# Compressed probabilities transposed two heads at a time, 512-column score matmuls, and a new order of the features in a hybrid decoder layer

## The chip, the cores and the metric

The kernel runs on one core of one Trainium2 chip, as one launch. The metric is device microseconds for that launch. The median of three timed runs of the kernel before is 698.51 us (698.43 to 698.52).

## What is computed

The reference is one decoder layer over 512 tokens of width 1024, in float32. The input is normalised and projected once (`w_in`). From the projection come a pooling mixer, an attention mixer and two sigmoid gates that merge them; then follow an output projection, a residual, a second norm, and a gated feed-forward layer with a causal convolution of width 3. The change lies in the attention mixer and in the features that run beside it:

```python
blk = kv[:, idx] + pe[None, None, :, None, :]                 # compress_blocks, for keys and for values
hid = jax.nn.silu(jnp.einsum('bnlgd,ldh->bngh', blk, w1))
return jnp.einsum('bngh,hd->bngd', hid, w2)
...
s = jnp.einsum('bqgrd,bngd->bgrqn', qc, kc) * scale           # 31 compressed keys
p_cmp = masked_softmax(s, cmp_end[None, :] <= t[:, None], -1)
o_cmp = jnp.einsum('bgrqn,bngd->bqgrd', p_cmp.astype(vc.dtype), vc)
...
out = gc[..., 0:1] * o_cmp + gc[..., 1:2] * o_sel + gc[..., 2:3] * o_win
```

There are eight query heads in two groups (`g`). At this length all eight selection blocks are chosen and the window covers everything, so the selected and the window branch are two causal attentions with keys and values of their own.

## The kernel before

Numbers are kept to float32 accuracy by splitting every operand into a rounded high part and a low rest, so that one product is three matmuls: high by high, high by low, low by high. TensorE is PE in the profile, VectorE DVE, ScalarE ACT, GpSimd POOL, and SyncE (SP) issues most DMAs.

**Order.** The kernel doesn't issue instructions as it is written. `Plan` (from line 112) records every operation with an estimated cost. `run` places them engine by engine, `dues` gives each a due time, and `emit` repeats this twelve times (TRIES) and issues the best order found. What comes out is a fixed order per engine; the semaphores between engines follow from the data alone. `pl.behind(op)` adds a dependency that only the planner knows: it moves an operation later in the order, but leaves no wait in the program. All operations pass through line 395 in the end, so the profile is read by tile names (`kt`, `cst`, `mm`), not by lines.

**Two streams.** TensorE work is in two streams that the planner interleaves. Stream "m" is the attention. Stream "f" (inside `with pl.on("f")`) is 22 features, the products of the normalised input with one 128-column slice of `w_in`. Each feature is 24 matmuls of 512 columns, shown as `mm<-xh,whi`, `mm<-xl,whi`, `mm<-xh,wlo`. Features need little of the other engines, so they fill TensorE while the attention waits for VectorE and ScalarE. They are two for the compression (`kc`), four for pooling (`pool_in`, each followed by a `mix`), eight pool gates (`gpy`, with four `pool_out` pairs) and eight attention gates (`thn`). A feature's weights come by an SP load into the ring `wraw` (three buffers), a ScalarE copy into `wlo`, an accumulating POOL DMA onto it, and a ScalarE copy into `whi`.

**The stage of the change.** After the first projections, `rope_split(t)` applies the rotary factors to the queries (`qp`) and keys (`kp`) of token tile t on VectorE and splits them into `qs` and `ks`; `qk_transpose(t)` transposes them on TensorE and ScalarE copies them out as `QT[g, t]` and `KT[0/1, t]` (high over low, and low over high). At the same time the two compression features give `kc` (four VectorE multiplications each), to which POOL adds the position terms, giving `kcb` (two additions each, 128x512). 64 matmuls with `w1` and two with `w2` follow, then a chain of small VectorE instructions (`kcx`, `kcm`, `kct`, `kcsp`), a transposition, and four copies into the zero-padded `kcz`. `cmp_scores` multiplies those with the queries, `cmp_softmax` makes the probabilities, and writes high part, low part and the high part again into `cst` (16 blocks of 3 x 32 columns, a tile for each group). `cmp_transpose(g, i)` transposes the four heads of one token tile into `PTc[g]`, 96 rows. In `av(h, 1)` one matmul multiplies the 96 rows with `vst`, 96 rows of compressed values.

**Scores.** `scores(h, i)` makes, for query tile i, the scores against key tiles 0 to i. For each key tile there are two matmuls of 256 columns (selected and window keys side by side), one against the high over low tile and one against the low over high one. The result goes into the two-bank tile `sc` where there are more than two key tiles, else into one of three `tr` banks.

Of the kernel before, what the change touches and what calls it, by code (L numbers as in the profile page):

```python
# [9 lines left out]
F32R = mybir.dt.float32r  # L10
# [5 lines left out]
P = 128  # L16
T = 512
# [381 lines left out]
def hybrid_layer(ctx: ExitStack, tc: tile.TileContext, xT, pos, par, cst, poolw, w1, wa, wb, wf,  # L399
# [23 lines left out]
    def bank(tag, shape=(P, T)):  # L423
        return pl.tile(ps, shape, F32, tag, tag, {"mm": 2, "tr": 3, "av": 1, "sc": 1}[tag], psum=True)
# [282 lines left out]
    def qk_transpose(t):  # L707
        for g in range(2):
            pt = bank("tr", (P, 4, P))
            with pl.unit():  # L710
                for i in range(4):
                    PE.transpose(pt[:, i], f32(qsp[t][g][:, i].rearrange("p a d -> p (a d)")), ident)
            QT[g, t] = page("qt", (P, 4, P), F32R)
            ACT.activation(QT[g, t], pt, AF.Copy)
        pt = bank("tr", (P, 2, 2, P))
        with pl.unit():
            for g in range(2):
                for b in range(2):
                    PE.transpose(pt[:, g, b], f32(ksp[t][:, 2 * b + g].rearrange("p a d -> p (a d)")), ident)
        KT[0, t], KT[1, t] = (page("kt", (P, 2, 2, P), F32R) for _ in range(2))  # L720
        ACT.activation(KT[0, t], pt, AF.Copy)
        ACT.activation(KT[1, t][0:64], pt[64:128], AF.Copy)
        ACT.activation(KT[1, t][64:128], pt[0:64], AF.Copy)

    rope_split(0)
    rope_split(1)
# [19 lines left out]
    pscale = R("pscale")  # L746
    yph, ypl, pooled = [], [], {}
    with pl.on("f"):
        for i in range(2):
            pt = feature(i, xh, xl)  # L750
            kc = page("kc", (P, 2, 256))
            for g in range(2):
                for q in range(2):
                    DVE.tensor_mul(kc[q * 64:(q + 1) * 64, g], pt[g * 64:(g + 1) * 64, q::2],
                                   rb[g * 64:(g + 1) * 64, q::2])
            for a in range(2):
                b = page("kcb", (P, 2, 32, 8))
                POOL.tensor_add(b.rearrange("p g n l -> p (g n) l"), kc.rearrange("p g (n l) -> p (g n) l", l=8),
                                pe[:, i, 8 * a:8 * a + 8][:, None, :].to_broadcast([P, 64, 8]))
                KC[i, a] = b  # L760
        def pool_in(gi):
# [36 lines left out]

        def pool_out(c):
            wh, wl = weights(wpo[c].rearrange("p a k n -> p (a k n)"), 1024)  # L800
            for f in (2 * c, 2 * c + 1):
                o = (f % 2) * 512
                pt = bank("mm")
                mm3(pt, wh[:, o:o + 512], wl[:, o:o + 512], yph, ypl, 0, 4)
                DVE.scalar_tensor_tensor(gpy[f], gpy[f], 1.0, pt, op0=ALU.add, op1=ALU.mult)
                SP.dma_start(gdr[f], gpy[f])

        pool_in(0)
        pw = page("pw", (P, 4, P))
        with pl.behind(turned[1]):  # L810
            SP.dma_start(pw, poolw)
        split(pwh, pwl, pw)
        for gi in range(1, 4):
            pool_in(gi)
            gate(thn, gi - 1, 14)
            mix(gi - 1)
        gate(thn, 3, 14)
        mix(3)
        for f in (0, 2):
            gate(gpy, f, 6)  # L820
            gate(gpy, f + 1, 6)
            pool_out(f // 2)
        gate(thn, 4, 14)
        for f in (4, 6):
            gate(gpy, f, 6)
            gate(gpy, f + 1, 6)
            pool_out(f // 2)
        for f in range(5, 8):
            gate(thn, f, 14)

    chid = []
    for i in range(2):
# [40 lines left out]
        for z in kcz.values():  # L873
            POOL.memset(f32(z), 0.0)
    pk = compress_out(1)
    vst = keep("vst", (96, 2, DH), F32R)
    for g in range(2):
        src = pk[g * 32:(g + 1) * 32, 0:64]
        for s in range(2):
            ACT.activation(vst[s * 32:(s + 1) * 32, g], src, AF.Copy, scale=0.5)  # L880
        DVE.scalar_tensor_tensor(vst[64:96, g], src, 0.5, f32(vst[g * 32:(g + 1) * 32, g]),
                                 op0=ALU.mult, op1=ALU.subtract)

    def compress_kt():
        pt = bank("tr")
# [11 lines left out]
    cps, cst_ = {}, {}  # L897
    PTc = {g: pl.tile(sb, (96, 4, T), F32R, "ptc", "ptc", 1) for g in range(2)}

    def cmp_scores(g):  # L900
        pt = bank("tr")
# [8 lines left out]
    def cmp_softmax(g):  # L910
        pt = bank("tr", (P, 4, P))
        with pl.unit():
            for hh in range(4):
                PE.transpose(pt[:, hh], cps[g][:, hh], ident)
        e = page("ce", (P, 16, 32))
        e4 = e.rearrange("p (h t) n -> p h (t n)", h=4)
        sm = keep("csm", (P, 3, 16), bufs=2)
        st = cst_[g] = keep("cst", (P, 16, 3, 32), F32R)
        DVE.tensor_add(e4, pt, C("cmask")[:, None, :].to_broadcast([P, 4, P]))
        DVE.tensor_reduce(sm[:, 0], e, axis=AX, op=ALU.min)  # L920
        DVE.tensor_sub(e, e, sm[:, 0][:, :, None].to_broadcast([P, 16, 32]))
        ACT.activation(e, e, AF.Exp, scale=-1.0)
        DVE.tensor_reduce(sm[:, 1], e, axis=AX, op=ALU.add)
        DVE.reciprocal(sm[:, 2], sm[:, 1])
        DVE.tensor_mul(sm[:, 2], sm[:, 2], vg[:, 4 * g:4 * g + 4].rearrange("p h t -> p (h t)"))
        DVE.tensor_mul(e, e, sm[:, 2][:, :, None].to_broadcast([P, 16, 32]))
        ACT.activation(st[:, :, 0], e, AF.Copy)
        ACT.activation(st[:, :, 2], e, AF.Copy)
        DVE.tensor_sub(st[:, :, 1], e, f32(st[:, :, 0]))

    def cmp_transpose(g, i):
        pt = bank("tr", (P, 4, P))
        with pl.unit():
            for hh in range(4):
                PE.transpose(pt[0:96, hh], f32(cst_[g][:, 4 * hh + i].rearrange("p a n -> p (a n)")), ident)
        ACT.activation(PTc[g][:, :, i * P:(i + 1) * P], pt[0:96], AF.Copy)

    Pt, PT, po, Oraw = {}, {}, {}, {}
    Oh = [page("oh", dt=F32R) for _ in range(4)]
# [2 lines left out]
    def scores(h, i):  # L942
# [1 line left out]
        n = i + 1  # L944
        pt = bank("sc", (P, 4, 2, P)) if n > 2 else bank("tr", (P, 2, 2, P))
        with pl.unit():
            for j in range(n):
                for s in range(2):
                    PE.matmul(pt[:, j], QT[g, i][:, hh], KT[s, j][:, g], start=(s == 0 and j % 2 == 0),
                              stop=(s == 1), skip_group_check=True)  # L950
        sm = keep("asm", (P, 4, 2), bufs=4)
        if n > 2:
            pp = [pl.tile(sb, (P, T), F32, "pp", "pp", 10)[:, :n * P].rearrange("p (j k) -> p j k", k=P) for _ in range(2)]
# [35 lines left out]
    def av(h, b):  # L989
# [4 lines left out]
        o = po[h]  # L994
        parts = [(0, 0, 0, 0), (1, 0, 1, 128), (2, 256, 2, 256), (2, 0, 3, 256)]
        if b == 1:
            PE.matmul(o[0:64], vst[:, g], PTc[g][:, h % 4], start=False, stop=False)
            parts = parts[::-1]
        for r, s, j, t0 in parts:
            n = 512 - t0  # L1000
# [433 lines left out]
```

## Time and profile before

| what | value |
|---|---|
| median of three runs | 698.51 us |
| the profiled execution's own time | 698.77 us |
| its span, first to last instruction | 697.0 us |
| DVE busy, share of the span | 481.1 us, 69% |
| ACT busy, share of the span | 436.3 us, 63% |
| POOL busy, share of the span | 103.3 us, 15% |
| granted TensorE clock | 1.00 throughout |
| HBM read and written | 70.27 MB, 6.29 MB |

Times inside the program are counted from the span's start. The stages that matter lie as follows: the first projections to about 54 us, the transpositions of queries and keys among the features to about 77 us, the compression to about 98 us, the attention interleaved with the features to about 270 us, a run of features alone to 284 us, then the merge and the feed-forward layer to the end.

A matmul's row gives its start and a duration that includes the way through the array; matmuls overlap, so the cost of one in a stream is the distance from its start to the next start. "x8" on a row of the timeline means that eight equal instructions are merged. The number in brackets is idle time of the engine before the row, and what ended it.

### The profile page before, as it was taken

What the parts mean: (1) busy time and instruction counts of PE and PEld (TensorE: products, weight loads), DVE (VectorE), ACT (ScalarE), POOL (GpSimd) and SP (SyncE); (2) the same over time, 40 slices, a digit from 0 to 9 for tenths busy, and PEclk for the clock granted to TensorE, in tenths of its full rate; (3) what the DMA queues carried; (4) which work ended last, traced back from release to release, by engine and by line L of the source; (5) the groups of instructions that cost most, each with busy time, mean ns of one, the idle gap of its engine ahead of it and who ended that gap; (6) DMA issues with size and microseconds to landing.
All of it is one profiled execution on the core that took longest, in us unless ns stands there. A gap on an engine that the chain in (4) does not pass through costs nothing.

```text
span 697.0 us, 11326 instructions
## 1 busy us (share of the span) xinstructions
PE 691.3 (99%) x4144; PEld 612.0 (88%) x4144; DVE 481.1 (69%) x1025; ACT 436.3 (63%) x798; POOL 103.3 (15%) x127
## 2 busy tenths in 40 slices
PE   9999999999999999999999999999999999999998
PEld 8898888888888888888888899999999999999987
DVE  5768678888866653685559977777766766776542
ACT  7667568767777663443359757768677766675320
POOL 0011400010011010000013223223122112220000
PEclk9999999999999999999999999999999999999999
DMA  8577344355655558744459787879978867864141
GB/s 297 171 177 207 96 111 107 106 137 122 166 136 152 151 126 240 272 164 136 151 144 233 168 214 174 215 169 198 225 189 180 196 162 168 182 158 108 46 128 61
DMA packets 45703, 113.99 MB, mean 164 GB/s; under 512 B 5328, under 2 KB 6096, under 8 KB 45648
## 3 DMA queue, kind: packets, MB, share of 16 engines
q1 hardware_dynamic: 29664, 76.57, 34.2%
q0 software_dynamic: 15840, 36.71, 29.2%
q8 instruction: 32, 0.52, 0.3%
q14 instruction: 23, 0.19, 0.1%
q10 hardware_dynamic: 144, 0.01, 0.0%
HBM read 70.27 MB, written 6.29 MB: 110 GB/s over the span
## 4 chain that ended last, share of the span: by engine, by line
PE 97%; DVE 2%; issue 0%; ACT 0%; POOL 0%; POOLq 0%
PE mm L395 41%; PE tr L395 31%; PE sc L395 14%; PE av L395 11%; DVE kp L395 1%; DVE kc L395 0%; DVE qp L395 0%; DVE th L395 0%; DVE qs L395 0%; DVE rt L395 0%; DVE ks L395 0%; DVE pml L395 0%; DVE o L395 0%; ACT ks L395 0%; POOL ones L395 0%
## 5 line engine op out<-in xcount | busy, mean ns | idle before, releaser
L395 ACT ACTIVATE whi<-wraw 128x1024 fp32r<-128x1024 f32 (+2 forms) x97 | 98.0, 1011 | 69.5 <-issue 24.6
L395 DVE TENSOR_TENSOR wlo<-wraw,whi 128x1024 fp32r<-128x1024 f32 (+1 forms) x66 | 76.3, 1158 | 16.9 <-ACT whi L395 14.9
L395 POOL DMA_DIRECT2D wlo<-wraw x30 | 26.3, 876 | 327.5 <-ACT wlo L395 257.9
L395 PE MATMUL mm<-xh,whi 128*128 128x512 f32 x176 | 73.0, 415 | 0.1
L395 PE MATMUL mm<-xh,wlo 128*128 128x512 f32 x176 | 69.0, 392 | 0.0
L395 PE MATMUL mm<-xl,whi 128*128 128x512 f32 x176 | 68.9, 392 | 0.0
L395 PE MATMUL mm<-tl,sh 128*128 128x256 f32 x190 | 53.5, 282 | 0.0
L395 PE MATMUL mm<-th,sl 128*128 128x256 f32 x174 | 49.1, 282 | 0.0
L395 PE MATMUL mm<-th,sh 128*128 128x256 f32 x174 | 49.0, 281 | 0.0
L395 ACT ACTIVATE wlo<-wraw 128x1024 fp32r<-128x1024 f32 x30 | 31.8, 1059 | 25.5 <-PE mm L395 16.6
L395 POOL DMA_DIRECT2D sl<-r x36 | 31.1, 863 | 88.0 <-ACT sl L395 66.1
L395 ACT ACTIVATE pp<-pp,asm 128x128 f32<-128x128 f32 (+3 forms) x64 | 35.4, 556 | 9.4 <-DVE asm L395 9.3
L395 PE MATMUL sc<-yh,whi 128*128 128x512 f32 x104 | 40.5, 389 | 0.0
L395 PE MATMUL sc<-yl,whi 128*128 128x512 f32 x104 | 40.5, 389 | 0.0
L395 PE MATMUL sc<-yh,wlo 128*128 128x512 f32 x104 | 40.5, 389 | 0.0
L395 PEld LDWEIGHTS mm<-xh,wlo 128*128 128x128 f32 x176 | 33.0, 188 | 7.5
L395 DVE SCALAR_TENSOR_TENSOR ft<-fg,pr,ft 128x511 f32<-128x511 f32 (+1 forms) x44 | 32.9, 749 | 9.5 <-ACT ft L395 8.8
L395 PEld LDWEIGHTS mm<-xh,whi 128*128 128x128 f32 x176 | 33.2, 188 | 4.7 <-DVE th L395 0.5
L395 PEld LDWEIGHTS mm<-xl,whi 128*128 128x128 f32 x176 | 33.3, 189 | 4.0
L395 PEld LDWEIGHTS mm<-tl,sh 128*128 128x128 f32 x190 | 35.7, 188 | 0.4
L395 PEld LDWEIGHTS mm<-th,sh 128*128 128x128 f32 x174 | 32.7, 188 | 1.1
L395 PEld LDWEIGHTS mm<-th,sl 128*128 128x128 f32 x174 | 32.7, 188 | 0.0
(397 smaller groups left out, 2100.6 us busy)
## 6 DMA issues: line engine op xcount, KB each, us to landing
wlo<-wraw POOLq DMA_DIRECT2D x30, 512.0 KB, 4.6
wraw<-wup SPq DMA_DIRECT2D x26, 512.0 KB, 3.9
wraw<-wf SPq DMA_DIRECT2D x22, 512.0 KB, 3.4
r<-wup SPq DMA_DIRECT2D x36, 256.0 KB, 5.4
sl<-r POOLq DMA_DIRECT2D x36, 256.0 KB, 5.4
wraw<-wdn SPq DMA_DIRECT2D x16, 512.0 KB, 3.7
sl<-s POOLq DMA_DIRECT2D x18, 256.0 KB, 5.5
sl<-wraw POOLq DMA_DIRECT2D x18, 256.0 KB, 4.2
```

The costliest lines, as they stand in the source:

```text
L395: getattr(self.real[o.eng], method)(*a, **kw)
```

## The change

Four things are changed, all before the merge:

- `cst` and `PTc` become one tile for both groups. `cst` holds high and low part once each (2 x 32 columns per head), and `cmp_transpose(g, b)` transposes two heads at a time, 128 rows, with b counting pairs of token tiles. The compressed values go into `vz`, 128 x 128 for each group and head of a pair, with the rows of the other head zero: eight small ScalarE copies and four VectorE instructions instead of four and two, and one POOL memset. The matmul in `av(h, 1)` gets 128 rows and 128 columns of weights instead of 96 and 64.
- Keys of two token tiles share one tile: `qk_transpose` transposes keys at odd t only, eight blocks, and `scores` takes two key tiles in one matmul of 512 columns where there are two.
- The four additions of the position terms are on VectorE instead of POOL, and for the planner behind the last key tile (`turned[3]`).
- The features have a new order: the compression's two stand behind a first attention gate, the other attention gates come between the pooling features, the pool gates and `pool_out` at the end.

```diff
-        pt = bank("tr", (P, 2, 2, P))
-        with pl.unit():
-            for g in range(2):
-                for b in range(2):
-                    PE.transpose(pt[:, g, b], f32(ksp[t][:, 2 * b + g].rearrange("p a d -> p (a d)")), ident)
-        KT[0, t], KT[1, t] = (page("kt", (P, 2, 2, P), F32R) for _ in range(2))
...
+        for g in range(2 if t % 2 else 0):
+            pt = bank("tr", (P, 2, 2, P))
+            with pl.unit():
+                for j in range(2):
+                    for b in range(2):
+                        PE.transpose(pt[:, j, b], f32(ksp[t - 1 + j][:, 2 * b + g].rearrange("p a d -> p (a d)")), ident)
+            hl, lh = (page("kt", (P, 2, 2, P), F32R) for _ in range(2))
+            KT[0, t // 2, g], KT[1, t // 2, g] = hl, lh
+            ACT.activation(hl, pt, AF.Copy)
+            ACT.activation(lh[0:64], pt[64:128], AF.Copy)
+            ACT.activation(lh[64:128], pt[0:64], AF.Copy)
...
-                POOL.tensor_add(b.rearrange("p g n l -> p (g n) l"), kc.rearrange("p g (n l) -> p (g n) l", l=8),
-                                pe[:, i, 8 * a:8 * a + 8][:, None, :].to_broadcast([P, 64, 8]))
+                with pl.behind(turned[3]):
+                    DVE.tensor_add(b.rearrange("p g n l -> p (g n) l"), kc.rearrange("p g (n l) -> p (g n) l", l=8),
+                                   pe[:, i, 8 * a:8 * a + 8][:, None, :].to_broadcast([P, 64, 8]))
...
+        gate(thn, 0, 14)
+        kv_in(0)
+        kv_in(1)
+        gate(thn, 1, 14)
         pool_in(0)
...
+        gate(thn, 2, 14)
         gate(thn, 3, 14)
+        pool_in(1)
+        mix(0)
...
+    with pl.behind(turned[2]):
+        POOL.memset(f32(ct[:, 2]), 0.0)
     for g in range(2):
         src = pk[g * 32:(g + 1) * 32, 0:64]
-        for s in range(2):
-            ACT.activation(vst[s * 32:(s + 1) * 32, g], src, AF.Copy, scale=0.5)
+        for r in range(4):
+            ACT.activation(vz[r * 32:(r + 1) * 32, g, r // 2, 0], src, AF.Copy, scale=0.5)
...
-        ACT.activation(st[:, :, 0], e, AF.Copy)
-        ACT.activation(st[:, :, 2], e, AF.Copy)
-        DVE.tensor_sub(st[:, :, 1], e, f32(st[:, :, 0]))
+        ACT.activation(hi, e, AF.Copy)
+        DVE.tensor_sub(lo, e, f32(hi))
...
+            for q in range(2):
+                for a in range(2):
+                    PE.transpose(pt[:, q, a], f32(cst_[:, 2 * b + a, 2 * q:2 * q + 2].rearrange("p h s n -> p (h s n)")), ident)
+        ACT.activation(PTc[:, 2 * g:2 * g + 2, 2 * b * P:2 * (b + 1) * P], pt.rearrange("p q a t -> p q (a t)"), AF.Copy)
...
-            for j in range(n):
+            for j in range(0, n, 2):
+                m = min(2, n - j)
                 for s in range(2):
-                    PE.matmul(pt[:, j], QT[g, i][:, hh], KT[s, j][:, g], start=(s == 0 and j % 2 == 0),
-                              stop=(s == 1), skip_group_check=True)
+                    PE.matmul(pt[:, j:j + m], QT[g, i][:, hh], KT[s, j // 2, g][:, 0:m], start=(s == 0), stop=(s == 1),
+                              skip_group_check=True)
...
-            PE.matmul(o[0:64], vst[:, g], PTc[g][:, h % 4], start=False, stop=False)
+            PE.matmul(o, vz[:, g, h % 2].rearrange("p s d -> p (s d)"), PTc[:, h // 2], start=False, stop=False)
...
-    extra = {(0, 2 * i + 2): (lambda i=i: cmp_transpose(0, i)) for i in range(NT)}
-    extra.update({(4, 2 * i): (lambda i=i: cmp_transpose(1, i)) for i in range(NT)})
+    extra = {(0, 4 * b + 2): (lambda b=b: cmp_transpose(0, b)) for b in range(2)}
+    extra.update({(4, 4 * b): (lambda b=b: cmp_transpose(1, b)) for b in range(2)})
```

From the merge on, TensorE's instructions stand in the same order in both programs.

More of the change, by code (lines that the diff above doesn't have):

```diff
@@ L714, in qk_transpose @@
             ACT.activation(QT[g, t], pt, AF.Copy)
-        pt = bank("tr", (P, 2, 2, P))
-        with pl.unit():
-            for g in range(2):
-                for b in range(2):
-                    PE.transpose(pt[:, g, b], f32(ksp[t][:, 2 * b + g].rearrange("p a d -> p (a d)")), ident)
-        KT[0, t], KT[1, t] = (page("kt", (P, 2, 2, P), F32R) for _ in range(2))
-        ACT.activation(KT[0, t], pt, AF.Copy)
-        ACT.activation(KT[1, t][0:64], pt[64:128], AF.Copy)
-        ACT.activation(KT[1, t][64:128], pt[0:64], AF.Copy)
+        for g in range(2 if t % 2 else 0):
[9 more added lines that the diff above has]
+            ACT.activation(lh[64:128], pt[0:64], AF.Copy)
     rope_split(0)
@@ L748, in hybrid_layer, with kv_in @@
     with pl.on("f"):
-        for i in range(2):
+        def kv_in(i):
             pt = feature(i, xh, xl)
@@ L812, in hybrid_layer @@
         split(pwh, pwl, pw)
[L813 to L816, printed above, removed]
+        gate(thn, 2, 14)
         gate(thn, 3, 14)
-        mix(3)
[L819 to L829, printed above, removed]
+        pool_in(1)
+        mix(0)
+        gate(thn, 4, 14)
+        gate(thn, 5, 14)
+        pool_in(2)
+        mix(1)
+        gate(thn, 6, 14)
+        gate(thn, 7, 14)
+        pool_in(3)
+        mix(2)
+        gate(gpy, 0, 6)
+        gate(gpy, 1, 6)
+        mix(3)
+        pool_out(0)
+        gate(gpy, 2, 6)
+        gate(gpy, 3, 6)
+        pool_out(1)
+        gate(gpy, 4, 6)
+        gate(gpy, 5, 6)
+        pool_out(2)
+        gate(gpy, 6, 6)
+        gate(gpy, 7, 6)
+        pool_out(3)
     chid = []
@@ L875, in hybrid_layer @@
     pk = compress_out(1)
-    vst = keep("vst", (96, 2, DH), F32R)
+    ct = keep("cst", (P, 3, T), F32R)
+    cst_ = ct[:, 0:2].rearrange("p a b -> p (a b)").rearrange("p (t h s n) -> p t h s n", t=4, h=4, s=2)
+    vz = ct[:, 2].rearrange("p (g r s d) -> p g r s d", g=2, r=2, s=2)
+    with pl.behind(turned[2]):
+        POOL.memset(f32(ct[:, 2]), 0.0)
     for g in range(2):
         src = pk[g * 32:(g + 1) * 32, 0:64]
-        for s in range(2):
-            ACT.activation(vst[s * 32:(s + 1) * 32, g], src, AF.Copy, scale=0.5)
-        DVE.scalar_tensor_tensor(vst[64:96, g], src, 0.5, f32(vst[g * 32:(g + 1) * 32, g]),
-                                 op0=ALU.mult, op1=ALU.subtract)
+        for r in range(4):
+            ACT.activation(vz[r * 32:(r + 1) * 32, g, r // 2, 0], src, AF.Copy, scale=0.5)
+        for r in range(2):
+            DVE.scalar_tensor_tensor(vz[r * 64:r * 64 + 32, g, r, 1], src, 0.5, f32(vz[g * 32:(g + 1) * 32, g, 0, 0]),
+                                     op0=ALU.mult, op1=ALU.subtract)
     def compress_kt():
@@ L895, in compress_kt @@
                                AF.Copy)
-    cps, cst_ = {}, {}
-    PTc = {g: pl.tile(sb, (96, 4, T), F32R, "ptc", "ptc", 1) for g in range(2)}
+    cps = {}
+    PTc = pl.tile(sb, (P, 4, T), F32R, "ptc", "ptc", 1)
     def cmp_scores(g):
@@ L917, in cmp_softmax @@
         sm = keep("csm", (P, 3, 16), bufs=2)
-        st = cst_[g] = keep("cst", (P, 16, 3, 32), F32R)
+        hi, lo = (cst_[:, :, :, s].rearrange("p t h n -> p h t n") for s in range(2))
         DVE.tensor_add(e4, pt, C("cmask")[:, None, :].to_broadcast([P, 4, P]))
@@ L926, in cmp_softmax, with cmp_transpose @@
         DVE.tensor_mul(e, e, sm[:, 2][:, :, None].to_broadcast([P, 16, 32]))
-        ACT.activation(st[:, :, 0], e, AF.Copy)
-        ACT.activation(st[:, :, 2], e, AF.Copy)
-        DVE.tensor_sub(st[:, :, 1], e, f32(st[:, :, 0]))
-    def cmp_transpose(g, i):
-        pt = bank("tr", (P, 4, P))
+        e = e.rearrange("p (h t) n -> p h t n", h=4)
+        ACT.activation(hi, e, AF.Copy)
+        DVE.tensor_sub(lo, e, f32(hi))
+    def cmp_transpose(g, b):
+        pt = bank("tr", (P, 2, 2, P))
         with pl.unit():
-            for hh in range(4):
-                PE.transpose(pt[0:96, hh], f32(cst_[g][:, 4 * hh + i].rearrange("p a n -> p (a n)")), ident)
-        ACT.activation(PTc[g][:, :, i * P:(i + 1) * P], pt[0:96], AF.Copy)
+            for q in range(2):
+                for a in range(2):
+                    PE.transpose(pt[:, q, a], f32(cst_[:, 2 * b + a, 2 * q:2 * q + 2].rearrange("p h s n -> p (h s n)")), ident)
+        ACT.activation(PTc[:, 2 * g:2 * g + 2, 2 * b * P:2 * (b + 1) * P], pt.rearrange("p q a t -> p q (a t)"), AF.Copy)
     Pt, PT, po, Oraw = {}, {}, {}, {}
```

## The prediction

> **What bounds the kernel now.** I read the page first, then the waits of TensorE, then busy time by stage.
>
> ```profile
> span 697.0 us, 11326 instructions
> PE 691.3 (99%) x4144; PEld 612.0 (88%) x4144; DVE 481.1 (69%) x1025; ACT 436.3 (63%) x798; POOL 103.3 (15%) x127
> ...
> PE 97%; DVE 2%; issue 0%; ACT 0%; POOL 0%; POOLq 0%
> ```
>
> TensorE is busy 99% of the span and carries 97% of the chain that ended last. So time is won in two ways only: fewer or shorter matmuls, or less of the 697.0 − 691.3 = 5.7 us in which TensorE is idle. The waits that the profile names:
>
> ```profile
> PE tr L395 <- DVE rt L395: 1.3, 1, 1.3
> PE mm L395 <- POOL ones L395: 1.0, 1, 1.0
> ```
>
> ```profile
> 98.00:145.00 47.00, 47.00 (x279) 40.77 (x279) 38.83 (x121) 35.26 (x80) 3.45 (x4) 1.00 0.41 102
> 145.00:270.00 125.00, 124.80 (x687) 104.56 (x686) 83.72 (x255) 86.29 (x175) 13.15 (x15) 1.00 0.58 147
> 270.00:697.00 427.00, 423.83 (x2618) 382.45 (x2616) 288.16 (x439) 249.84 (x421) 72.49 (x84) 1.00 0.68 171
> ```
>
> The second wait is the start of the program, untouched. The first lies in the stage of the change. The windows (length, then busy time of PE, PEld, DVE, ACT and POOL, granted clock, DMA share, GB/s) show the attention without idle TensorE: 47.00 of 47.00 and 124.80 of 125.00 us. The 3.2 us after 270 us belong to the feed-forward part, whose TensorE order the change leaves alone. So what can be gained is the one wait plus matmul time, and everything else that changes is a risk of new waits.
>
> **The wait at 72 us, and what makes it.** Timelines of TensorE, VectorE and GpSimd:
>
> ```profile
> 72.08 0.39 PE L395 MATMUL mm<-xh,wlo 128*128 128x512 f32 x1
> 73.81 0.41 PE L395 MATMUL tr<-cs,qs 128*128 128x128 f32 x2 [1.35 <-DVE rt L395]
> ```
>
> ```profile
> 61.89 0.42 DVE L395 TENSOR_TENSOR kp<-kp,gkv 128x256 f32<-128x256 f32 x1
> ...
> 67.05 1.19 DVE L395 TENSOR_TENSOR kp<-kp,rt 128x64 f32<-128x64 f32 x1
> ...
> 70.79 2.31 DVE L395 TENSOR_TENSOR kp<-kp,gkv 128x256 f32<-128x256 f32 x1
> ...
> 73.25 0.42 DVE L395 TENSOR_TENSOR qs<-qp,qs 128x256 fp32r<-128x256 f32 x1
> ...
> 74.07 0.22 DVE L395 TENSOR_TENSOR kp<-kp,rt 128x64 f32<-128x64 f32 x1
> ...
> 77.02 1.15 DVE L395 TENSOR_TENSOR vg<-gates,cs 128x32 f32<-128x32 f32 x1
> ```
>
> ```profile
> 66.84 1.32 POOL L395 TENSOR_TENSOR kcb<-kc,pr 128x512 f32<-128x512 f32 x1 [2.21 <-DVE kc L395]
> ...
> 71.22 1.60 POOL L395 TENSOR_TENSOR kcb<-kc,pr 128x512 f32<-128x512 f32 x1
> 72.45 1.76 POOL L395 MEMSET kcz<- 128x512 f32 x3
> 76.82 2.52 POOL L395 TENSOR_TENSOR kcb<-kc,pr 128x512 f32<-128x512 f32 x2 [2.61 <-DVE kc L395]
> ```
>
> TensorE waits for `qs`, which VectorE made at 73.25. Ahead of it the multiplication of `kp` took 2.31 us; the same shape took 0.42 at 61.89. It ends at 73.10, just after GpSimd's addition (71.22 + 1.60 = 72.82). The final addition of `kp` took 1.19 instead of 0.22 and ends at 68.24, after the other addition at 68.16; `vg` is a third. Each time a VectorE instruction with two SBUF inputs is held until the GpSimd addition is over. The two before the wait cost 1.89 + 0.97 = 2.86 us of VectorE. With `qs` that much earlier, the idle 1.35 us are gone; counted in starts, 73.81 − 72.08 − 0.23 = 1.50 us.
>
> The Trainium skill states the same as an exclusive lock, and says that a two-input VectorE instruction loses only against a GpSimd instruction that reads SBUF (SBUF — State Buffer, section "SBUF: two separate sides"). By that rule the new memset of `vz` cannot hold VectorE, and the trace agrees: the instructions at 73.25 and 74.07 keep their 0.42 and 0.22 us beside the memsets of 72.45. Were the rule wrong for memsets, the added one would cost at most its own length.
>
> **Terms of the sum.** Spacing is read from the start of a row to the start of the next.
>
> ```profile
> 94.42 3.79 PE L395 MATMUL tr<-qt,kcz 128*128 128x512 f32 x16
> 98.05 0.64 PE L395 MATMUL tr<-kt,qt 128*128 128x256 f32 x4
> ...
> 101.74 1.12 PE L395 MATMUL sc<-kt,qt 128*128 128x256 f32 x8
> 102.69 0.40 PE L395 MATMUL mm<-xh,whi 128*128 128x512 f32 x1
> ...
> 114.15 0.60 PE L395 MATMUL tr<-cs,cst 128*96 128x128 f32 x4
> 114.51 0.47 PE L395 MATMUL mm<-xh,whi 128*128 128x512 f32 x1
> 114.82 0.39 PE L395 MATMUL mm<-xl,whi 128*128 128x512 f32 x1
> 115.05 0.39 PE L395 MATMUL mm<-xh,wlo 128*128 128x512 f32 x1
> ```
>
> ```profile
> L395 PE MATMUL sc<-kt,qt 128*128 128x256 f32 x112 | 16.1, 284 | 0.0
> L395 PE MATMUL tr<-kt,qt 128*128 128x256 f32 x48 | 8.6, 287 | 0.0
> L395 PE MATMUL tr<-cs,cst 128*96 128x128 f32 x32 | 4.8, 272 | 0.0
> L395 PE MATMUL tr<-cs,qs 128*128 128x128 f32 x32 | 4.5, 273 | 1.3 <-DVE rt L395 1.3
> ```
>
> 1. Transpositions of the probabilities: 32 become 16. Four of them and the 512-column matmul behind take 114.82 − 114.15 = 0.67 us, less 0.23 for the latter (115.05 − 114.82) leaves 0.44, or 0.11 each. Sixteen fewer save **1.75 us**. The width grows from 96 to 128; the query transpositions, of 128 rows, have the same duration (273 ns on average against 272), so the rest cost no more.
> 2. Scores: 112 + 48 = 160 matmuls of 256 columns become 64 of 512 and 32 of 256. Eight of 256 take 102.69 − 101.74 = 0.95 us, 0.119 each. One of 512 takes (98.05 − 94.42)/16 = 0.227 at best and 0.23 among the features. A merged pair saves 0.238 − 0.23 = 0.008 to 0.238 − 0.227 = 0.011 us; 64 pairs save 0.5 to 0.7, and I take **0.6 us**. The lower bound is nothing, if wider moving tiles stream no faster per column.
> 3. The wait at 72 us: **1.5 us**, bounds 0 and 1.5.
> 4. The matmul with `vz` streams 512 columns as with `vst`, the key transpositions remain 16: nothing.
>
> The Trainium skill's formula for the gap between isolated matmuls, N/2.4 + 2.5 ns (TensorE: Matmul & The Clock Gate, section "Back-to-back issue gap"), would make the merge worth 2.5 ns a pair, 0.16 us in all; the spacing here is 10 ns above it for 256 columns. The difference of 0.4 us lies inside the range.
>
> What is added elsewhere, and its cover. Counts for the changed program are from the order in which its instructions stand on each engine.
>
> ```profile
> L395 DVE TENSOR_TENSOR ps<-u 128x511 f32<-128x511 f32 x4 | 2.7, 686 | 0.1
> L395 DVE TENSOR_TENSOR kc<-mm,rb 64x256 f32<-64x256 f32 x8 | 3.4, 420 | 0.1
> L395 ACT ACTIVATE ptc<-tr 96x512 fp32r<-96x512 f32 x8 | 4.8, 595 | 1.9 <-PE tr L395 1.9
> L395 ACT ACTIVATE cst<-ce 128x512 fp32r<-128x512 f32 x4 | 2.3, 620 | 0.0
> L395 ACT ACTIVATE vst<-tr 32x64 fp32r<-32x64 f32 x4 | 0.9, 214 | 1.7 <-PE tr L395 1.6
> ```
>
> - The four additions on VectorE have the size of `ps<-u`: 0.69 us each, 2.7 in all, against some 3.8 that VectorE loses to GpSimd now (2.86, and 0.9 on `vg`). In the changed order they stand behind all rotary work and have no wait on `turned[3]`. What waits for them are the products with `w1`. Ahead of the first 16 products TensorE has the last eight key transpositions and nine feature matmuls, 0.88 + 2.07 us; VectorE has in that time two `kc` multiplications, the gates and two additions, about 0.84 + 0.4 + 1.4 = 2.6. Ahead of the second group it has those 16 products (1.8 us) and six feature matmuls (1.4), against four `kc` multiplications and the first addition (1.7 + 0.7). Both are hidden, by 0.3 to 0.8 us.
> - The compression's chain. It runs from the first product with `w2` to the transposition of `kcsp`:
>
> ```profile
> 85.32 0.33 PE L395 MATMUL tr<-pr,hid 128*64 128x64 f32 x2
> ...
> 92.42 0.33 PE L395 MATMUL tr<-cs,kcsp 64*128 64x64 f32 x2
> ```
>
> ```profile
> 90.12 0.28 DVE L395 TENSOR_TENSOR kcsp<-kcx,kcsp 64x128 fp32r<-64x128 f32 x1
> ```
>
>   The chain takes 90.40 − 85.32 = 5.1 us and TensorE 7.1, so it has 2.0 to spare. The new order puts 24 feature matmuls there instead of 27, which takes 0.7 off. Still hidden, by about 1.2 us; if not, each late us costs one. ScalarE's four more `vz` copies (0.9 us) stand in it too, two ahead of `kcsp` on VectorE as before.
> - ScalarE is relieved of four copies of `ptc` and two of `cst`: 6 x 0.6 = 3.6 us, nothing on the path.
> - The features' order moves pooling work (four to seven long VectorE instructions of 0.69 us a feature) later. On SP, stores of `tdr` now stand among the weight loads; each waits for a tanh that is done several matmuls before. The last two `gdr` stores come right before the merge and are read only at its end, some 20 us later: hidden.
>
> Sum: 1.75 + 0.6 + 1.5 = 3.85 us. The profiled execution took 698.77 us (span 697.0 and 1.8 around it), so 694.9 by its own clock; the median of the runs is 0.26 below it: **694.7 us**.
>
> **The rivals.**
> - *The wait moves.* TensorE's order is fixed, so a small error in a tight cover becomes a stall: the second additions, the `kcsp` chain, or the high and low parts of `pz`, each with 0.2 to 1.2 us to spare. For it: 1.50 us were lost at 72 us in an order that was made to avoid just that. Against it: in 172 us of attention the same kind of order lost only 0.2. The matmul savings stay, the 1.5 us are given back: 698.5 − 2.3 = 696.2 us.
> - *Merging does nothing.* The 64 wide matmuls take 0.238 each: 695.3 us; inside the range.
> - *VectorE sets the end (slower).* Pooling moves into 98 to 145 us, where VectorE is busy 38.83 of 47.00 us. Its room is 8.2 us. Beyond it, every further us delays softmax and so TensorE. A result 0.2% above before needs 3.85 + 1.4 = 5.3 us of new waits, so 13.5 us more VectorE work there: 699.9 us. A pooling feature has at most 7 x 0.69 = 4.8 us, so nearly three would have to be added and no gate leave. For it: VectorE works in bursts, so it can decide before the average is full. Against it: gates leave the stretch in exchange, and 145 to 270 us has 41 us of room.
> - *No change at all.* The two first terms are given back by waits: about 698.
>
> **How the numbers follow.** Forecast 62% (694.7, own range 693.7 to 695.7); the wait moves 20%; merging nothing 5%; no change 5%; VectorE sets the end 8%. What this measurement can tell from no change is about 0.2%, 1.4 us, so faster means below 697.1: 0.62 + 0.20 + 0.05 = 0.87; same 0.05; slower 0.08. The range: downwards the best terms (1.75 + 0.7 + 1.5, and up to 0.9 if the third hold, 1.15 us on `vg`, delays TensorE in a way that the waits don't name) give 693.6; upwards the moved wait with 0.8 us more gives 697.0.
>
> **What would show it right or wrong.** Right: no idle TensorE at 70 to 76 us; `kp` multiplications at 0.42 us throughout and no GpSimd additions; 16 transpositions of `cst`; score matmuls of 512 columns at a spacing of 0.23; TensorE's busy time lower by about 2.3 us. Wrong: a wait for `kcb`, `kcsp`, `kcz`, `pz` or `pt` among TensorE's waits, or VectorE busy over nine tenths between 85 and 150 us.

## The result, and the profile after

The changed kernel takes 693.55 us (median of 6 runs, 692.48 to 694.01) against 698.47 (698.31 to 698.87) before it: ratio 0.9927, with a 95% interval of 0.9914 to 0.9939. That is 4.92 us faster. The profiled execution took 693.65 us.

The page after, with the span, the engines and the chain of work that ended last:

```profile
span 691.9 us, 11152 instructions
PE 687.2 (99%) x4064; PEld 606.2 (88%) x4064; DVE 479.3 (69%) x1031; ACT 433.6 (63%) x796; POOL 98.3 (14%) x124
...
PE 97%; DMA 1%; ACT 1%; SPq 0%; issue 0%; DVE 0%
```

TensorE still sets the end, with 80 matmuls fewer and 4.1 us less of busy time (691.3 to 687.2). The whole list of TensorE's waits after:

```profile
PE mm L395 <- POOL ones L395: 1.0, 1, 1.0
PE tr L395 <- ACT xh L395: 0.4, 1, 0.4
```

The wait for `rt` at 72 us is gone, and no wait for `kcb`, `kcsp`, `kcz`, `pz` or `pt` has come. To see where the time went I cut the program at two points that every kernel here has: the first transposition of a query, and the first matmul of the merge. TensorE's timeline, before and then after (start, duration):

```profile
54.49 0.60 PE L395 MATMUL tr<-cs,qs 128*128 128x128 f32 x4
...
284.21 0.39 PE L395 MATMUL tr<-oh,whi 128*128 128x512 f32 x1
```

```profile
54.26 1.04 PE L395 MATMUL tr<-cs,qs 128*128 128x128 f32 x8
...
279.12 0.39 PE L395 MATMUL tr<-oh,whi 128*128 128x512 f32 x1
```

The stage between took 229.72 us before and 224.86 after: 4.86 us less. What lies behind it, 697.0 − 284.21 and 691.9 − 279.12, is 412.8 in both, and the start is 0.23 us shorter, which is within its scatter between executions (below). So what was won was won in the stage of the change. The groups that answer to the terms of the sum (count, then total and mean ns of one):

```profile
L395 PE MATMUL sc<-kt,qt 128*128 128x512 f32 x48 | 13.7, 392 | 0.0
L395 PE MATMUL tr<-kt,qt 128*128 128x512 f32 x16 | 5.1, 397 | 0.0
...
L395 PE MATMUL tr<-cs,cst 128*128 128x128 f32 x16 | 2.4, 272 | 0.0
...
L395 DVE TENSOR_TENSOR kcb<-kc,pr 128x512 f32<-128x512 f32 x4 | 2.6, 685 | 0.0
L395 DVE TENSOR_TENSOR kp<-kp,gkv 128x256 f32<-128x256 f32 x4 | 1.5, 418 | 0.0
```

Every `kp` multiplication now takes 0.42 us. I then summed, over the stage, the distances from the start of each matmul to the next start, by kind of matmul:

| where | before, us | after, us | less by | forecast |
|---|---|---|---|---|
| wait at 72 us | 1.50 | 0 | 1.50 | 1.5 |
| transpositions of `cst` (32, then 16) | 2.92 | 1.42 | 1.50 | 1.75, with the next row |
| wide matmuls right behind a block of transpositions, above 0.23 each | 4.45 | 4.24 | 0.21 | |
| scores (160, then 96) | 19.48 | 18.87 | 0.61 | 0.6 |
| four longer distances at two mixes | 0.74 | 0 | 0.74 | nothing |
| all else | | | 0.30 | nothing |
| sum | | | 4.86 | 3.85 |

The sums are of rows with two decimals and good to some 0.05 us: the scores give 18.87 here and 18.93 in a second execution of the same program (e10). The fifth row is what I had missed. TensorE's timeline at the third and fourth mix, before; then the weight loads of the same place (idle time of the loads in brackets), before:

```profile
145.44 0.39 PE L395 MATMUL mm<-pmh,pwl 128*128 128x512 f32 x1
145.93 0.50 PE L395 MATMUL mm<-xh,whi 128*128 128x512 f32 x1
146.27 0.40 PE L395 MATMUL mm<-xl,whi 128*128 128x512 f32 x1
...
153.28 0.48 PE L395 MATMUL mm<-pmh,pwh 128*128 128x512 f32 x1
153.86 0.50 PE L395 MATMUL mm<-pml,pwh 128*128 128x512 f32 x1
154.20 0.39 PE L395 MATMUL mm<-pmh,pwl 128*128 128x512 f32 x1
```

```profile
145.93 0.19 PEld L395 LDWEIGHTS mm<-xh,whi 128*128 128x128 f32 x1 [0.53 <-DVE th L395]
...
153.86 0.19 PEld L395 LDWEIGHTS mm<-pml,pwh 128*128 128x128 f32 x1 [0.41 <-DVE pml L395]
```

Matmuls of 512 columns follow each other at 0.23 us, or 0.32 right behind transpositions. Here the distances are 0.49 and 0.34, then 0.58 and 0.34, which is 0.26 + 0.11 + 0.26 + 0.11 = 0.74 us too long. No row of TensorE has a bracket, because a matmul's row lasts 0.39 to 0.50 and covers the first 0.16 to 0.27 us of any gap behind its 0.23. What is left uncovered, 145.93 − 145.44 − 0.39 and 153.86 − 153.28 − 0.48, is 0.10 twice: just the 0.20 us of idle time that I had read as the whole loss. The rows of the weight loads do have one. The first load waits for `th`, VectorE's reading of the gate feature just ahead of the mix, whose bank it frees; the second waits for `pml`, the low part of what the mix takes in (`pmh` is the high part). After the change a mix runs at 0.23 and 0.22:

```profile
129.45 0.39 PE L395 MATMUL mm<-pmh,pwh 128*128 128x512 f32 x1
129.68 0.39 PE L395 MATMUL mm<-pml,pwh 128*128 128x512 f32 x1
129.90 0.39 PE L395 MATMUL mm<-pmh,pwl 128*128 128x512 f32 x1
```

`pml` of the fourth mix, VectorE before and then after:

```profile
153.13 0.68 DVE L395 TENSOR_TENSOR pml<-pm,pmh 128x512 fp32r<-128x512 f32 x1
```

```profile
197.98 0.69 DVE L395 TENSOR_TENSOR pml<-pm,pmh 128x512 fp32r<-128x512 f32 x1 [0.22 <-ACT pmh L395]
```

Before, it is ready at 153.81, behind the start of its mix at 153.28. After, it is ready at 198.67, 3.8 us ahead of its mix at 202.50. Counted from the end of VectorE's first reading of the fourth pooling feature (`u`, at 139.45 and at 185.50), TensorE reached the mix after 13.8 us before and after 17.0 us now, while VectorE needed 14.4 and 13.2 us to `pml`.

### The profile page after: what moved, and what is told of

It reads as the page before. It is cut to its first block, busy times and chain, and to the rows that moved or that the text cites. A ratio compares the mean times of both kernels' runs of the same rounds, so it can differ in the third digit from the quotient of the medians.

```text
span 691.9 us, 11152 instructions
## 1 busy us (share of the span) xinstructions
PE 687.2 (99%) x4064; PEld 606.2 (88%) x4064; DVE 479.3 (69%) x1031; ACT 433.6 (63%) x796; POOL 98.3 (14%) x124
## 4 chain that ended last, share of the span: by engine, by line
PE 97%; DMA 1%; ACT 1%; SPq 0%; issue 0%; DVE 0%
PE mm L395 42%; PE tr L395 31%; PE sc L395 13%; PE av L395 11%; DMA wraw<-wa 1%; SPq L395 0%; ACT xh L395 0%; ACT sq L395 0%; ACT whi L395 0%; ACT acc L395 0%; DVE o L395 0%
## 5 line engine op out<-in xcount | busy, mean ns | idle before, releaser
L395 ACT ACTIVATE pp<-pp,asm 128x384 f32<-128x384 f32 (+3 forms) x64 | 35.5, 557 | 5.8 <-DVE asm L395 5.8
```

What stands on the lines that cost most here:

```text
L395: getattr(self.real[o.eng], method)(*a, **kw)
```

## The experiments

All kernels at a glance: medians beside the kernel before on the same chip (698.56, 698.46 and 698.24 us in the three groups), and the three pieces of each profiled execution, cut as above.

| kernel | us | ratio, 95% | start | stage | to the end |
|---|---|---|---|---|---|
| before | 698.47 | | 54.49 | 229.72 | 412.77 |
| e1 transpositions alone | 696.32 | 0.9967 [0.9955, 0.9980] | 54.14 | 226.33 | 414.13 |
| e2 scores alone | 697.65 | 0.9986 [0.9977, 0.9995] | 53.49 | 228.16 | 416.74 |
| e3 additions alone | 697.79 | 0.9990 [0.9981, 0.9999] | 54.20 | 229.21 | 412.79 |
| e4 new order alone | 696.35 | 0.9969 [0.9958, 0.9981] | 54.44 | 227.62 | 412.74 |
| e5 additions, every order kept | 696.92 | 0.9979 [0.9969, 0.9988] | 54.73 | 228.18 | 412.75 |
| e6 changed, old order | 696.57 | 0.9971 [0.9961, 0.9981] | 54.56 | 226.92 | 414.11 |
| e7 changed, old matmuls | 696.42 | 0.9968 [0.9956, 0.9980] | 54.16 | 227.66 | 412.78 |
| e8 later part of the order | 697.88 | 0.9995 [0.9985, 1.0004] | 53.45 | 229.11 | 412.80 |
| e9 changed, additions on GpSimd | 693.41 | 0.9932 [0.9919, 0.9946] | 53.68 | 224.87 | 412.75 |
| e10 changed | 693.42 | 0.9932 [0.9919, 0.9944] | 54.03 | 224.86 | 412.75 |

The start varies by 1.3 us between executions (53.45 to 54.73) with no pattern that follows the edits, so I read the stage. Each stage is read from one execution; the changed kernel was profiled twice, and its stage took 224.86 us both times.

**e1: only the transposition of probabilities, two heads at a time.**

```diff
-                PE.transpose(pt[0:96, hh], f32(cst_[g][:, 4 * hh + i].rearrange("p a n -> p (a n)")), ident)
-        ACT.activation(PTc[g][:, :, i * P:(i + 1) * P], pt[0:96], AF.Copy)
+                    PE.transpose(pt[:, q, a], f32(cst_[:, 2 * b + a, 2 * q:2 * q + 2].rearrange("p h s n -> p (h s n)")), ident)
+        ACT.activation(PTc[:, 2 * g:2 * g + 2, 2 * b * P:2 * (b + 1) * P], pt.rearrange("p q a t -> p q (a t)"), AF.Copy)
```

> Only the probabilities' part of the change (cst, PTc, vz, transpositions of two heads). Theory (the terms add up): 16 transpositions fewer at 0.11 us, 1.75 us; the wait at 72 us on VectorE stays, so about 696.7 us. Rival (matmul work is given back by waits, and the whole gain is the end of waits): within 0.5 us of before, 698.0 or more. The planner makes a new order for each kernel, so waits at the mixes may differ by up to 1 us either way.

The `cst` class fell from 2.92 to 1.41 us, as in the changed kernel. But the stage lost 3.39, because the planner had made another order of everything and the wait at 72 us had gone with it. The time of 696.32 us is near the 696.7 expected by luck: the stage lost 1.6 us more than the sum said, and the piece behind it took 1.36 us more. VectorE in e1: held are no longer `kp` instructions but a multiplication of `qp` (1.39 us, beside an addition of 66.81 to 68.33) and `vg`, and TensorE waits for neither.

```profile
67.09 1.39 DVE L395 TENSOR_TENSOR qp<-qp,gq 128x128 f32<-128x128 f32 x1
...
69.82 0.42 DVE L395 TENSOR_TENSOR kp<-kp,gkv 128x256 f32<-128x256 f32 x1
...
78.18 0.20 DVE L395 TENSOR_SCALAR gates<-gates 128x96 f32<-128x96 f32 x1
78.42 1.92 DVE L395 TENSOR_TENSOR vg<-gates,cs 128x32 f32<-128x32 f32 x1
```

**e2: only the key tiles in pairs and the scores of 512 columns.**

```diff
-            for j in range(n):
+            for j in range(0, n, 2):
+                m = min(2, n - j)
...
-                    PE.matmul(pt[:, j], QT[g, i][:, hh], KT[s, j][:, g], start=(s == 0 and j % 2 == 0),
+                    PE.matmul(pt[:, j:j + m], QT[g, i][:, hh], KT[s, j // 2, g][:, 0:m], start=(s == 0), stop=(s == 1),
```

> Only the key tiles in pairs and the score matmuls of 512 columns. Theory: 64 merged pairs at 0.009 us, 0.6 us, so about 697.9 us with the wait at 72 us still there. Rival (wide matmuls stream no faster per column): 698.5 us, and the spacing of a 512-column score matmul is 0.238 us.

The scores took 18.79 us instead of 19.48: 0.69 less. Here too the new order of the planner ended the wait at 72 us, but the three kinds of matmul of the mixes took 4.12 us against 3.55 before, so the stage lost 1.56. Behind the stage the profiled execution, at 700.16 us the longest of the eleven of e2, lost 4 us; the last section comes back to that. e1 and e2 showed that a part cannot be weighed by building it alone, since the planner answers each edit with another order. The next runs hold the order, or change it alone.

**e3: only the additions on VectorE, behind the last key tile.**

```diff
-                POOL.tensor_add(b.rearrange("p g n l -> p (g n) l"), kc.rearrange("p g (n l) -> p (g n) l", l=8),
...
+                with pl.behind(turned[3]):
+                    DVE.tensor_add(b.rearrange("p g n l -> p (g n) l"), kc.rearrange("p g (n l) -> p (g n) l", l=8),
```

> Only the four additions on VectorE instead of GpSimd, features in the old order. Theory (GpSimd's additions hold VectorE's rotary instructions, and this is the wait at 72 us): the wait of 1.5 us is gone, the kp multiplications take 0.42 us each, about 697.0 us. Rival (the features' order ended the wait, since it puts the compression behind a gate): the wait or another of the same size stays, 698.3 us or more.

The wait at 72 us went, as expected, but only 0.51 us of the stage. TensorE in e3 shows where the rest was given back, at the fourth mix:

```profile
152.04 0.49 PE L395 MATMUL mm<-pmh,pwh 128*128 128x512 f32 x1 [0.63 <-ACT pmh L395]
152.82 0.50 PE L395 MATMUL mm<-pml,pwh 128*128 128x512 f32 x1 [0.28 <-DVE pml L395]
```

The second is the matmul that comes late in the kernel before too, where only the weight loads show it; the first, which waits for `pmh`, was not late there. My rival "the wait moves" fits this kernel, but at a place that it had not named.

**e4: only the new order of the features; the additions stay on GpSimd.**

```diff
+        gate(thn, 0, 14)
+        kv_in(0)
+        kv_in(1)
+        gate(thn, 1, 14)
         pool_in(0)
...
+        pool_in(1)
+        mix(0)
```

> Only the new order of the features, additions still on GpSimd. Theory: the two waits at the mixes (0.35 us for the bank at 146 us, 0.35 and 0.11 us for pml at 154 us, by distances between starts) go, but GpSimd's additions still hold VectorE instructions of 0.2 to 0.4 us to 1.2 us or more, somewhere later: 697.6 us, between 696.5 and 698.5. Rival (the order ended the wait at 72 us too): no TensorE wait between 55 and 100 us, 696.1 us.

The rival was right. The order alone ends the wait at 72 us and all the waits at the mixes, with GpSimd's additions still there: the stage lost 2.10 us. VectorE's groups in e4: the hold has fallen on `vg`, at 1.17 us, while the `kp` multiplications keep 0.42.

```profile
L395 DVE TENSOR_TENSOR kp<-kp,gkv 128x256 f32<-128x256 f32 x4 | 1.7, 421 | 0.1
...
L395 DVE TENSOR_TENSOR vg<-gates,cs 128x32 f32<-128x32 f32 x1 | 1.2, 1165 | 0.0
```

**e5: the kernel before with its order on every engine, and only the four additions issued on VectorE.**

```diff
-                getattr(self.real[o.eng], method)(*a, **kw)
+                getattr(self.real["DVE" if o.eng == "POOL" and method == "tensor_add" else o.eng], method)(*a, **kw)
```

> The kernel before, planned as before, so that every engine keeps its order; only the four additions are issued on VectorE, at the places that the plan gave them. TensorE's order is the same to the instruction. Theory (GpSimd's additions hold VectorE, and this makes the wait at 72 us): ahead of the late qs stands one addition of 0.69 us in place of 2.86 us of holds, so qs comes 2.2 us earlier, the 1.5 us wait is gone, the waits at the mixes (146 and 154 us) stay: 697.0 us. Rival (another order ends the wait, not the engine): the wait stays, 698.3 us or more.

This is the test of what makes the wait, with nothing else moved. VectorE in e5, at the place where the same multiplication took 2.31 us:

```profile
68.15 0.68 DVE L395 TENSOR_TENSOR kcb<-kc,pr 128x512 f32<-128x512 f32 x1
...
70.66 0.42 DVE L395 TENSOR_TENSOR kp<-kp,gkv 128x256 f32<-128x256 f32 x1
```

The wait at 72 us is gone and the stage is 1.54 us shorter, so GpSimd's additions were a necessary part of it. How the hold begins stays open: in the kernel before, the row of the held multiplication starts at 70.79 and that of the addition at 71.22, which should have left it its 0.42 us. The waits at the mixes are untouched, as TensorE's timeline shows by the same distances as before, 0.49 and 0.58:

```profile
144.12 0.39 PE L395 MATMUL mm<-pmh,pwl 128*128 128x512 f32 x1
144.61 0.50 PE L395 MATMUL mm<-xh,whi 128*128 128x512 f32 x1
...
151.98 0.48 PE L395 MATMUL mm<-pmh,pwh 128*128 128x512 f32 x1
152.56 0.51 PE L395 MATMUL mm<-pml,pwh 128*128 128x512 f32 x1
```

**e6: the changed kernel with the features in their old order.**

```diff
-        gate(thn, 0, 14)
-        kv_in(0)
-        kv_in(1)
-        gate(thn, 1, 14)
         pool_in(0)
...
-        gate(thn, 2, 14)
+        for gi in range(1, 4):
+            pool_in(gi)
+            gate(thn, gi - 1, 14)
+            mix(gi - 1)
         gate(thn, 3, 14)
```

> The changed kernel with the features in the old order (additions on VectorE, both matmul parts kept). Theory (the 1.1 us that my sum lacked are waits at the mixes, which the features' order ends): waits of 0.7 to 1.6 us at the mixes, from pml or the bank, and 694.6 us, between 694.2 and 695.2. Rival (the 1.1 us came with the additions or the matmuls): 693.6 us.

The expected time was missed by 2 us, and the rival's by 3. In the stage the old order costs 2.06 us (226.92 against 224.86), most of it at the mixes. In e6 the weight load of the fourth mix's first matmul alone has 0.84 us:

```profile
151.74 0.19 PEld L395 LDWEIGHTS mm<-pmh,pwh 128*128 128x128 f32 x1 [0.84 <-ACT pmh L395]
```

Another 1.36 us came behind the stage. So the new order took about 2.1 us from the stage in both settings, beside the old matmuls (e4) and beside the new ones (e6). That the two figures agree is chance: in e4 the order ends the wait at 72 us (1.50) and the four distances at the mixes (0.74); in e6 there is no wait at 72 us, and the planner's plan with the old order loses about 2.1 us at the mixes instead of 0.74.

**e7: the changed kernel with the old transpositions and the old scores.** It has the code of the kernel before in the places of e1 and e2, with the new order and the additions on VectorE.

```diff
-            for j in range(0, n, 2):
-                m = min(2, n - j)
+            for j in range(n):
...
-            PE.matmul(o, vz[:, g, h % 2].rearrange("p s d -> p (s d)"), PTc[:, h // 2], start=False, stop=False)
+            PE.matmul(o[0:64], vst[:, g], PTc[g][:, h % 4], start=False, stop=False)
```

> The changed kernel without its two matmul parts: old transpositions and old score matmuls, new features' order, additions on VectorE. Theory: TensorE has 1.75 + 0.6 us more work and no new waits: 695.9 us, and the stretch from the first query transposition to the first merge matmul is 2.35 us longer than in the changed kernel. Rival (the matmul parts shorten waits as well): 696.4 us or more.

At 696.42 us the kernel is 0.5 us slower than the theory said, and at the bound that I had given the rival. The stage is 2.80 us longer than in the changed kernel, not 2.35: 1.50 in the class of `cst`, some 0.4 in the scores, 0.19 in one wait ahead of the products with `w1`, and the rest in the wide matmuls behind transpositions and spread over the others. Its stage is that of e4 to 0.04 us. Since e4 differs from it only in the engine and the late place of the additions, this edit adds nothing to the new order.

**e8: the kernel before with the compression's two features first, as before, and the other features in the new order.** The additions stay on GpSimd.

```diff
+        kv_in(0)
+        kv_in(1)
+        gate(thn, 0, 14)
+        gate(thn, 1, 14)
         pool_in(0)
```

> The kernel before with only the later part of the new features' order: the compression's two features first, as before, then gates between the pooling features and pool_out at the end; additions on GpSimd, old matmuls. Theory: no waits at the mixes (0.9 us less), while GpSimd's additions fall beside the rotary work again and the wait at 72 us may or may not stay, as the planner places it: 697.7 us with it, 696.3 us without. Rival (it is the compression's place that ends the mix waits): 698.5 us with waits at the mixes.

The waits at the mixes went, the wait at 72 us stayed. Rows of e8 from the timelines of TensorE, VectorE and GpSimd:

```profile
71.06 0.39 PE L395 MATMUL mm<-xh,wlo 128*128 128x512 f32 x1
72.78 0.63 PE L395 MATMUL tr<-cs,qs 128*128 128x128 f32 x4 [1.33 <-DVE rt L395]
```

```profile
69.76 2.31 DVE L395 TENSOR_TENSOR kp<-kp,gkv 128x256 f32<-128x256 f32 x1
```

```profile
70.17 1.61 POOL L395 TENSOR_TENSOR kcb<-kc,pr 128x512 f32<-128x512 f32 x1
```

The distance 72.78 − 71.06 − 0.23 is 1.49 us, with the same multiplication held to 2.31 us as before. So two places in the order have two effects. One attention gate ahead of the compression takes the additions away from the rotary work; the rest of the new order ends the waits for `pml` and `th` at the mixes. Whether the features' sequence does the latter, or the other attention matmuls that the planner lays around the mixes with it, no run separates.

**e9 and e10: the changed kernel, once with the additions issued on GpSimd and every order kept, and once as it is.**

```diff
-                getattr(self.real[o.eng], method)(*a, **kw)
+                getattr(self.real["POOL" if method == "tensor_add" and "kcb" in a[0].tensor.name else o.eng], method)(*a, **kw)
```

> The changed kernel with its own plan, every order kept; only the four additions are issued on GpSimd again. They now stand behind the rotary work. Theory (the additions' engine is worth 1.5 us only where they meet rotary instructions that TensorE waits for): the additions of 1.3 us each hold only kc, the gates or vg; TensorE waits at most about 0.8 us for the last kcb before the second group of products with w1: 693.6 to 694.4 us. Rival (moving the additions to VectorE is worth its 1.5 us in any order): 695.0 us.

> The changed kernel itself, beside the one before on the same chip: 693.55 us as measured first, within 0.5 us.

693.41 and 693.42 us, stages 224.87 and 224.86. The rival's 695.0 falls. The engine of the additions is worth nothing once the order is new. GpSimd and VectorE in e9 show why the additions no longer hurt:

```profile
74.94 1.61 POOL L395 TENSOR_TENSOR kcb<-kc,pr 128x512 f32<-128x512 f32 x1
```

```profile
72.41 0.21 DVE L395 TENSOR_TENSOR vg<-gates,cs 128x32 f32<-128x32 f32 x1
...
75.67 1.73 DVE L395 TENSOR_TENSOR kc<-mm,rb 64x256 f32<-64x256 f32 x4 [3.05 <-PE mm L395]
```

All rotary work is over by then. What stands beside the addition of 74.94 to 76.55 are the first three of four `kc` multiplications, which read PSUM and one SBUF tile; the four take 1.73 / 4 = 0.43 us each, as ever.

No version beat the changed kernel; e9 equals it.

## Why the prediction was wrong by 1.15 us

One way through the runs adds up without a rest: from the kernel before to the new order (e4) the stage lost 2.10 us, from there to the new matmuls and the additions' late place (e9) 2.75, and from there to VectorE's additions (e10) 0.01. Together they make the 4.86. The forecast for the same steps was 1.5 for order and additions together and 2.35 for the matmuls.

- **The step that failed is the features' order, put at nothing.** I wrote that it only moves pooling work later, and that the attention lost no more than 0.2 us in 172, from windows with TensorE busy 47.00 of 47.00 and 124.80 of 125.00 us. But a matmul's row covers the start of a gap. By distances between starts the two mixes lost 0.74 us in that stretch. The order ends these waits: they stay in e5, grow in e3 and e6, which have the old order, and are gone in e4 and e8. The 0.74 us are most of the 1.01 that the sum of 3.85 lacked in the stage; 0.30 is spread (below). The Trainium skill says that the busy share of matmuls is a bad measure of how near TensorE is to its limit, since matmuls are pipelined, and names the work done and the busy share of the weight loads instead (Perfetto Trace Analysis, section "Identifying the Most-Contended Engine"). The rows here agree that it is a bad measure: the weight loads have a gap of 0.53 us where the matmuls' rows leave 0.10.
- **The wait at 72 us: right in place and size, half right in cause.** It was worth 1.50 us, and e5 shows that it takes GpSimd's additions. But I credited the move to VectorE. In this kernel it also takes the early place of the compression, and either cure is enough: the engine alone (e5) or the order alone (e4). In the new order the engine is worth 0.01 us.
- **Transpositions: right.** Forecast 1.75; measured 1.50 in their own distances and 0.21 in the wide matmuls behind them.
- **Scores: right in kind, a little high in size.** Forecast 0.6, with bounds of 0.5 and 0.7; 0.61 in the changed kernel and 0.69 in e2, where the order changed as well. In e4, with the new order and the old scores, they took 19.29 us instead of 19.48, so some 0.2 of the 0.61 came with the order. Merging alone is worth some 0.4 (e4 to e9, and e7). "Merging does nothing" falls.
- **The matmuls as a whole** gave 2.75 us on the way from e4 to e9, against 2.35. The classes explain 1.50 + 0.34 + 0.42 = 2.26 of that. The rest, and the 0.30 of the first table, is spread over hundreds of matmuls. Of the 0.30, by the trace's unrounded starts, 0.08 lie in 160 transpositions of `pp`, 0.08 in 64 `av<-pt,vv` and 0.11 in 64 matmuls of `pool_out`, 0.0005 to 0.002 us each; what causes them stays open.
- **TensorE's busy time** fell by 4.1 us, not by the 2.3 that I gave as a sign. 3.3 of it lie in the stage: the matmuls, the 0.30, and the parts of the gaps that the rows had covered, 0.54 at the mixes and 0.15 at 72 us.
- **What I called hidden was hidden.** The row of `kcsp` on VectorE and its transposition on TensorE after:

```profile
90.13 0.28 DVE L395 TENSOR_TENSOR kcsp<-kcx,kcsp 64x128 fp32r<-64x128 f32 x1
```

```profile
91.25 0.33 PE L395 MATMUL tr<-cs,kcsp 64*128 64x64 f32 x2
```

  It had 0.84 us to spare where I had 1.2. The tight covers of my likeliest rival held in the planned order. What another plan broke in e3 and e6 was none of those that I had listed, but `pmh` and `pml` at the mixes.
- **VectorE does not set the end.** The stretches of busy time (PE, PEld, DVE, ACT, POOL) after:

```profile
98.00:145.00 47.00, 47.00 (x252) 39.72 (x251) 39.13 (x126) 35.97 (x82) 4.30 (x5) 1.00 0.43 106
145.00:270.00 125.00, 125.00 (x645) 103.47 (x644) 88.73 (x260) 85.25 (x172) 12.04 (x14) 1.00 0.60 152
```

  39.13 of 47.00 us is 83%, close to the 38.83 before and under the nine tenths that I had named.
- **The range.** Its lower end, 693.6, was built from the best terms and `vg`, which gave nothing. The result lies 0.05 us under it. That the lower end came so near is luck: the true reserve was at the mixes, and I had no term for it.

## What to carry to other kernels

Where TensorE is busy 99% of the time, short waits hardly appear in its busy time, its idle time or its list of waits (0.20 of 0.74 us here): read the distances between starts, and the weight loads' waits, before calling a stage free of loss. A change of order can be worth as much as the arithmetic that it comes with, so price it by listing every short wait that it could end, and not only those that it could make. Where a planner makes the order anew after each edit, parts built alone do not add up (e1 to e4 took 3.39 + 1.56 + 0.51 + 2.10 = 7.56 us from the stage, all of them together 4.86); keep the order fixed and change one thing, or change the order alone.

## What I had not expected

- **A wait far behind the change.** In e1, e2 and e6 the piece from the merge to the end is 1.3 to 4.0 us longer, though the edits end before it. In all three TensorE waits there for ScalarE's `u`, 1.07, 2.21 and 1.04 us; in e1 ScalarE had itself waited for a load some 10 us earlier. Rows of e1, TensorE and then ScalarE:

```profile
523.92 0.39 PE L395 MATMUL mm<-th,sh 128*128 128x256 f32 x1 [1.07 <-ACT u L395]
```

```profile
513.87 0.63 ACT L395 ACTIVATE sl<-wraw 128x512 fp32r<-128x512 f32 x1 [3.38 <-DMA sl<-r]
...
523.51 0.37 ACT L395 ACTIVATE u<-mm 128x256 f32<-128x256 f32 x1
```

  That the planner's new order of GpSimd and SP causes the late load is my reading; no run separates it. In e2 the granted clock fell right behind that wait, as its windows show (the figure behind the five engines), and matmuls of 256 columns followed each other at 0.21 us instead of 0.12:

```profile
525.00:530.00 5.00, 3.76 (x16) 3.57 (x17) 4.31 (x8) 4.32 (x9) 1.72 (x2) 0.66 1.02 268
```

- **One SBUF input may be held too.** In e2 an instruction with a single tensor input took 1.55 us, beside GpSimd additions of 73.58 to 76.52. VectorE and GpSimd in e2:

```profile
75.32 1.55 DVE L395 TENSOR_SCALAR gates<-gates 128x96 f32<-128x96 f32 x1
```

```profile
73.58 2.94 POOL L395 TENSOR_TENSOR kcb<-kc,pr 128x512 f32<-128x512 f32 x2 [3.14 <-DVE kc L395]
```

  The same shape took 0.20 us in e1 (at 78.18, shown there), at a time without an addition. It is one row, and no run was made for it. I had counted only instructions with two SBUF inputs as exposed. The Trainium skill names a second case for the lock, VectorE's modes that use two ports (SBUF — State Buffer, section "SBUF: two separate sides"); whether this instruction ran in such a mode no run here shows.
